# Tensor work of GpSimd moved to VectorE and ScalarE in a two-block transformer kernel, with paired matmul operands

## Chip, cores and metric

One core of one Trainium2 chip. The time is the device time of the core in microseconds (us). A change is read from the median of several runs; the stretches and waits are read from one profiled execution.

## The reference, cut to what matters

A model of two blocks over 256 tokens of width 1024, all inputs and results in float32. The first block has two layers with modulation by `c`: layer 0 with latent attention and retention over 512 tokens (256 of them context), layer 1 with an S5 state-space scan. The second has two layers, each with a gated feed-forward, a hybrid mixer (pooling and sparse attention) and a second feed-forward.

```python
def squared_relu_mlp(h, w1, w2):
    return jnp.square(jax.nn.relu(h @ w1)) @ w2
def swiglu(x, w_gate, w_up, w_down):
    return (jax.nn.silu(x @ w_gate) * (x @ w_up)) @ w_down
...
# first_block, layer l = 0, 1
    o_c, o_l = mla_retention_mixer(...) if l == 0 else s5_mixer(...)
    x = x + mod_l[:, 2] * o_l
    x = x + mod_l[:, 5] * squared_relu_mlp(h_l, mlp_w1[l], mlp_w2[l])
...
# second_block, layer l = 0, 1
    x = layer_norm(ALPHA * x + 0.5 * swiglu(x, ffn1...), ln1_g[l], ln1_b[l])
    x = layer_norm(ALPHA * x + hybrid_mixer(x, ...), ln2_g[l], ln2_b[l])
    x = layer_norm(ALPHA * x + 0.5 * swiglu(x, ffn2...), ln3_g[l], ln3_b[l])
```

## The kernel before, in words

Activations lie transposed: features on partitions, in 8 tiles of 128, tokens along the free axis. Weights come in units of 128 x 1024 float32 (512 KB, "raw"), each loaded by one DMA on SP's queue (L350, up to six ahead). For a product that keeps float32's accuracy each operand is split in two parts that the matmul engine takes: for a weight ScalarE casts the high part `whi` (L365) and the low part is `wlo = raw - whi` (L370); for an activation there are `xh` and `xl` in two tiles. `mm3` (L333) then issues three matmuls into one PSUM tile: `whi` with `xh`, `whi` with `xl`, `wlo` with `xh`. In a trace the stationary operand is the second name: `ps<-xl,whi`.

`wlo` is made on VectorE, or on GpSimd while the counter `s.n_pool` is above 0. It is set in four places: to 6 at the start, to 8 after the first pair of the first MLP (`fmulg`, L396) and after the first pair of each "raw" row of units (`raw_mul`, L437), to 7 in the hybrid mixer.

The raw row bridges a layer norm: while the norm's sums are still being made, PE multiplies the first eight units with the unnormalised activations (two more columns, 258, carry the correction), and `raw_norm` (L476, L477) corrects the result. `layernorm` (L1837) then makes per feature tile `lt`, `xh`, `xl` (L1868 to L1872) and, on GpSimd, `ax = ALPHA * y` (L1873) for the residual.

`ffn` (L1903) goes over 22 pairs of gate and up units: two products into two PSUM tiles, tanh on ScalarE, two VectorE operations (L1925, L1926), and a split into `hdh`, `hdl` (L719). Then eight output tiles of 22 products each, added to the residual in `resid` (L1888), whose sums over features go through `colacc` (L621), an add on GpSimd.

In layer 0 `l0_attn` (L993) makes, per head, a decay table for each of two shifts (`ret_table`) and the scores of retention (`ret_score`, a matmul with 64 rows). In layer 1 `s5_prep` makes norm sums, and eight scans run: `scan` multiplies by rotations (L1736, L1737), adds (L1740; one of the four adds on GpSimd), runs the recurrence (L1719) and in `post` rotates back on GpSimd (L1696 to L1699; the second half of the last scan on VectorE). `output` needs the matrices `s5km`, made earlier and kept in DRAM: 16 loads of 128 KB for its first part and 32 of 64 KB for its second, all on SP's queue (L1633); the second part's lie in buffers of `whi` and `wlo`.

The order of the instructions on each engine is set by a scheduler from the order in which the code is written and the buffers that are free; each engine then runs its own list in order.

Of the kernel before, what the change touches and what calls it, by code (L numbers as in the profile page):

```python
# [9 lines left out]
F32 = mybir.dt.float32  # L10
# [9 lines left out]
KT = D // 128  # L20
# [9 lines left out]
POOL_UNITS = 8  # L30
POOL_START = 6
# [7 lines left out]
POOL_ATT = 7  # L39
# [5 lines left out]
Z_POOL = (0, 1),  # L45
# [247 lines left out]

class K:
    def __init__(s, tc, A, out, voff, coff, ctx, dbg=None):
# [13 lines left out]
        s.n_dma = s.n_prep = s.n_use = s.n_pool = 0  # L309
# [48 lines left out]
    def _prep(s, i):  # L358
# [78 lines left out]
    def raw_mul(s, units):  # L437

        hi, lo, _ = s.xr
        for i in range(0, len(units), 2):  # L440
            w = [s.unit(*u) for u in units[i:i + 2]]
            ps = [s.ps([128, S + 2]) for _ in w]
            for k in range(KT):
                if i == 0 and k == KT - 1:
                    s.n_pool = POOL_UNITS
# [248 lines left out]
    def modnorm_raw(s, mk, x, st):  # L694
# [8 lines left out]
        out = [(mk(), mk()) for _ in range(KT)]  # L703
# [13 lines left out]
    def split(s, src, h, lw):  # L717
        s.nc.scalar.copy(h, src)
        s.nc.vector.tensor_tensor(lw, src, h, op=OP.subtract)  # L719
        return h, lw  # L720


    def layer0(s):
# [6 lines left out]
        with ExitStack() as es:  # L730
            slab = es.enter_context(tc.tile_pool(name="slab", bufs=43))
# [47 lines left out]
    def l0_proj(s, es, mx, x, halves):  # L779
# [9 lines left out]
        s.n_pool = POOL_START  # L789
# [94 lines left out]
        slab = es.enter_context(tc.tile_pool(name="slabq", bufs=9))  # L884
        s.rq, s.rk, s.sg = [], [], []
        for i in range(4, 12):
# [8 lines left out]
            nc.gpsimd.tensor_tensor(sh, sh, rs, op=OP.mult)  # L895
            V.tensor_tensor(dst[:, 0:S], dst[:, 0:S], rc, op=OP.mult)
            V.tensor_tensor(dst[:, 0:S], dst[:, 0:S], sh, op=OP.add)
            if i == 5:
# [3 lines left out]
                for n in range(3):  # L902
# [3 lines left out]
                    zs.append(s.split(zc[n], s.r2(), s.r2()))  # L906
# [30 lines left out]
        for hp in range(4):  # L937
# [5 lines left out]
            for a in range(2):  # L943
# [4 lines left out]
                nc.gpsimd.tensor_copy(k_[R], s.kr[R])  # L948
# [44 lines left out]
    def l0_attn(s, mx):  # L993
# [4 lines left out]
        dj = lambda jt: dd[:, 128 * (1 - jt):128 * (1 - jt) + S]  # L998
# [3 lines left out]
        def ret_table(h):  # L1002

            lf, lb = s.lg[:, 0, h:h + 1], s.lg[:, 0, 8 + h:9 + h]
            nb = s.lg[:, 1, 8 + h:9 + h]
            bf, bb = s.lg[:, 2, h:h + 1], s.lg[:, 2, 8 + h:9 + h]
            tbs[h] = []
            for jt in range(2):
                tb = s.r2(F32)
                t1 = s.sq.tile([128, S], F32, name="rt1", tag="shf")  # L1010
                t2 = s.sq.tile([128, S], F32, name="rt2", tag="rt2")
                V.tensor_scalar(t1, dj(jt), lf, None, op0=OP.mult)
                V.scalar_tensor_tensor(t1, in0=dj(jt), scalar=nb, in1=t1, op0=OP.mult, op1=OP.min)
                nc.scalar.activation(tb[:, S:], t1, AF.Exp)
                nc.scalar.activation(tb[:, 0:S], dj(jt), AF.Exp, scale=lf, bias=bf)
                nc.scalar.activation(t2, dj(jt), AF.Exp, scale=nb, bias=bb)
                nc.gpsimd.tensor_tensor(tb[:, 0:S], tb[:, 0:S], t2, op=OP.add)
                tbs[h].append(tb)

        def ret_score(h, jt):  # L1020
            hp, a = divmod(h, 2)
            r = slice(64 * a, 64 * a + 64)
            n = T2 if jt >= 2 else S
            ps = s.ps()
            s.mm(ps[:, :n], s.rk[hp][r, jt * 128:(jt + 1) * 128], s.rq[hp][r, :n])
# [44 lines left out]
        def mla_pv(hp):  # L1070
# [8 lines left out]
            ohl[hp] = s.split(po, s.r2(), s.r2())  # L1079
# [31 lines left out]
        for hp in range(4):  # L1111
# [7 lines left out]
            ohl[4 + hp] = s.split(s.sg[hp], s.r2(), s.r2())  # L1119
# [3 lines left out]
    def mlp(s, l, x, T, halves, fill=iter(()), st=None):  # L1123
        nc, tc = s.nc, s.tc
        m = s.mod[l]
        with ExitStack() as es:
# [4 lines left out]
            hp = eh.enter_context(tc.tile_pool(name="hm", bufs=16))  # L1131
            mk = lambda: hp.tile([128, T], F32R, name="hm", tag="hm")
# [8 lines left out]
            for c in range(32 // nf):  # L1141
                hid = []
                for f in range(nf):
# [9 lines left out]
                    elif l == 0 and c == 0 and f < 2:  # L1153
# [3 lines left out]
                        ps = first[f]  # L1157
                    else:
# [50 lines left out]
                for d in range(KT if l else 0):  # L1209
                    ps = s.ps()  # L1210
                    for f in range(nf):
# [3 lines left out]
                        s.mm3(ps[:, :T], (hi[:, o:o + 128], lo[:, o:o + 128]), hid[f], f == 0, f == nf - 1)  # L1215
                    for c0, c1, mi in halves:
                        nc.vector.scalar_tensor_tensor(x[:, d, c0:c1], in0=ps[:, c0:c1], scalar=m[:, 5, d, mi:mi + 1],
                                                       in1=x[:, d, c0:c1], op0=OP.mult, op1=OP.add)
# [1197 lines left out]
```

## Time and profile before

| | us |
|---|---|
| median of 3 runs | 2234.01 (2230.95 to 2234.57) |
| the profiled execution | 2235.03 |
| its span | 2233.2 |
| PE busy in it | 2050.1 (92%) |
| VectorE (DVE) busy | 1548.9 (69%) |
| ScalarE (ACT) busy | 996.7 (45%) |
| GpSimd (POOL) busy | 426.7 (19%) |

The span is the time from the first to the last instruction in the trace; 1.8 us lie around it. "Busy" counts the time in which at least one instruction of the engine runs. In a timeline a row stands for one instruction or for several of a kind that follow each other (xN), with its start, the time it took, and in brackets how long the engine had been idle and what it waited for. PEclk is the clock granted to the matmul engine as a share of full speed, 2.4 GHz; its lower level is 0.5.

### The profile page before, as it was taken

The numbers are of one execution on the slowest core, as the hardware profiler recorded it, in microseconds if no ns is written. First come the engines' busy times: TensorE is split into PE (matmuls) and PEld (weight loads), VectorE is DVE, ScalarE is ACT, GpSimd is POOL, SyncE is SP. The second block draws the span as 40 slices with busy tenths as digits, with TensorE's granted clock in tenths as the row PEclk, the third lists the DMA queues.
The fourth block names the chain that finished last, engine by engine and source line by source line (L and its number), as shares of the span: only waits on it lengthen the run. The fifth ranks groups of instructions, "written<-read, shape, count | busy, mean of one in ns | idle before, by whom it ended". The sixth has DMA issues, their size and how long they took to land. (4 is left out here: it accounts for less than half of the span.)

```text
span 2233.2 us, 39543 instructions
## 1 busy us (share of the span) xinstructions
PE 2050.1 (92%) x15641; PEld 1765.2 (79%) x15641; DVE 1548.9 (69%) x2880; ACT 996.7 (45%) x1808; POOL 426.7 (19%) x363
## 2 busy tenths in 40 slices
PE   6999998799997986899999998998999999798998
PEld 4774365577775875799999997788998999768996
DVE  6877666999873459775546558867658666878655
ACT  3443543233332343467434444545445444554443
POOL 2020114200000015540000024252024003426000
PEclk8999998899999997899999999999999999999999
DMA  7323433576778347245555555235553556314553
GB/s 292 109 78 125 158 105 131 188 214 223 237 231 251 125 160 247 99 160 192 185 183 182 180 191 160 86 104 167 184 198 133 192 192 200 127 39 170 189 182 121
DMA packets 137434, 373.67 MB, mean 167 GB/s; under 512 B 12896, under 2 KB 43552, under 8 KB 136736
## 3 DMA queue, kind: packets, MB, share of 16 engines
q1 hardware_dynamic: 137248, 371.14, 50.4%
q8 instruction: 123, 2.02, 0.4%
q14 instruction: 63, 0.52, 0.1%
HBM read 345.33 MB, written 25.76 MB: 166 GB/s over the span
## 5 line engine op out<-in xcount | busy, mean ns | idle before, releaser
L365 ACT CAST whi<-raw 128x1024 fp32r<-128x1024 f32 (+1 forms) x491 | 510.7, 1044 | 641.5 <-PE ps L323 406.9
L370 DVE TENSOR_TENSOR wlo<-raw,whi 128x1024 fp32r<-128x1024 f32 (+1 forms) x407 | 507.6, 1248 | 391.0 <-ACT whi L365 390.9
L323 PE MATMUL ps<-xl,whi 128*128 128x256 f32 x1312 | 375.2, 286 | 12.2 <-DVE xl L1872 12.2
L323 PE MATMUL ps<-xh,whi 128*128 128x256 f32 x1312 | 379.1, 289 | 3.5 <-ACT whi L365 2.5
L323 PE MATMUL ps<-xh,wlo 128*128 128x256 f32 x1312 | 372.2, 284 | 2.8 <-POOL wlo L370 2.8
L323 PEld LDWEIGHTS ps<-xl,whi 128*128 128x128 f32 x1312 | 251.4, 192 | 16.3 <-DVE xl L1872 14.6
L370 POOL TENSOR_TENSOR wlo<-raw,whi 128x1024 fp32r<-128x1024 f32 (+1 forms) x84 | 214.0, 2561 | 236.0 <-ACT whi L365 132.1
L323 PEld LDWEIGHTS ps<-xh,whi 128*128 128x128 f32 x1312 | 251.5, 192 | 7.4 <-ACT whi L365 3.3
L323 PEld LDWEIGHTS ps<-xh,wlo 128*128 128x128 f32 x1312 | 251.1, 192 | 3.5 <-POOL wlo L370 3.5
L323 PE MATMUL ps<-hm,whi 128*128 128x512 f32 (+1 forms) x896 | 231.4, 350 | 0.4 <-ACT lt L1497 0.4
L323 PE MATMUL ps<-hidh,whi 128*128 128x512 f32 (+1 forms) x512 | 174.8, 345 | 12.2 <-ACT whi L365 11.0
L323 PEld LDWEIGHTS ps<-hm,whi 128*128 128x128 f32 x896 | 155.6, 190 | 29.2 <-issue 3.1
L323 PE MATMUL ps<-hidl,whi 128*128 128x512 f32 (+1 forms) x512 | 174.7, 341 | 2.3 <-DVE hidl L719 2.1
L323 PE MATMUL ps<-hidh,wlo 128*128 128x512 f32 (+1 forms) x512 | 172.5, 338 | 0.0
L323 PE MATMUL ps<-hm,wlo 128*128 128x512 f32 (+1 forms) x448 | 155.0, 346 | 5.0 <-POOL wlo L370 5.0
L323 PE MATMUL ps<-hdl,whi 128*128 128x256 f32 x528 | 149.1, 283 | 0.0
L323 PE MATMUL ps<-hdh,whi 128*128 128x256 f32 x528 | 148.5, 282 | 0.0
L323 PE MATMUL ps<-hdh,wlo 128*128 128x256 f32 x528 | 148.4, 281 | 0.0
L323 PE MATMUL ps<-slab,whi 128*128 128x512 f32 x416 | 133.1, 399 | 1.5 <-ACT slabq L931 1.5
L323 PEld LDWEIGHTS ps<-hidh,whi 128*128 128x128 f32 x512 | 97.0, 190 | 27.1 <-ACT whi L365 11.9
L323 PE MATMUL ps<-xrh,whi 128*128 128x258 f32 x384 | 110.6, 290 | 0.0
L323 PE MATMUL ps<-xrl,whi 128*128 128x258 f32 x384 | 109.4, 287 | 0.0
(539 smaller groups left out, 4313.9 us busy)
## 6 DMA issues: line engine op xcount, KB each, us to landing
raw<-in_m_dram SPq DMA_DIRECT2D x128, 512.0 KB, 4.3
raw<-in_f1gu_dram SPq DMA_DIRECT2D x88, 512.0 KB, 3.5
raw<-in_f2gu_dram SPq DMA_DIRECT2D x88, 512.0 KB, 3.7
raw<-in_ada_dram SPq DMA_DIRECT2D x80, 512.0 KB, 4.3
raw<-in_f1d_dram SPq DMA_DIRECT2D x44, 512.0 KB, 3.8
raw<-in_f2d_dram SPq DMA_DIRECT2D x44, 512.0 KB, 3.7
raw<-in_ni_dram SPq DMA_DIRECT2D x24, 512.0 KB, 3.5
slab<-in_adaq_dram SPq DMA_DIRECT2D x32, 256.0 KB, 6.2
```

Source lines behind the costliest of these rows:

```text
L323: s.last = s.nc.tensor.matmul(out, lhsT, rhs, start=start, stop=stop)
L365: nc.scalar.copy(hi[:, :w], raw[:, :w])
L370: eng.tensor_tensor(lo[:, :w], raw[:, :w], hi[:, :w], op=OP.subtract)
```

## The change

1. All `wlo` are made on VectorE; the counter goes. `colacc`, the sums of `s5_prep`, the scan's add and `post`, the rotary products and the decay table's add go from GpSimd to VectorE. `ax`, a copy of the rotary keys and two fills of `s5M` go to ScalarE.
2. `xh` and `xl` of an activation lie side by side in one tile (`HL`). Where the PSUM tile has three dimensions, `mm3` issues one 512-column matmul of `whi` with both and one of 256 columns of `wlo` with `xh`; the two halves are added afterwards, by `both` (a ScalarE copy and a VectorE add) or by two residual operations. This holds for the gate and up units that are not raw, for the down projections but the last feed-forward's, and for the second MLP's units from the ninth on with its down projection. Layer 0, the raw units, the projections and the last down projection stay as they were.
3. In layer 0 both shifts' decay tables are one tile, made for one head in one set of operations, and `ret_score` issues the matmuls of a pair of heads one after the other.
4. The loads of `s5km` go from SP's queue to GpSimd's.

```diff
     def mm3(s, out, w, x, start, stop):
+        if len(out.shape) == 3:
+
+            s.mm(out, w[0], x.both, start, False)
+            s.mm(out[:, 0], w[1], x[0], False, stop)
+            return
...
-        eng = nc.gpsimd if s.n_pool > 0 else nc.vector
-        s.n_pool -= 1
-        eng.tensor_tensor(lo[:, :w], raw[:, :w], hi[:, :w], op=OP.subtract)
+        nc.vector.tensor_tensor(lo[:, :w], raw[:, :w], hi[:, :w], op=OP.subtract)
...
-            s.nc.gpsimd.tensor_tensor(acc[0], acc[1] if d == 1 else acc[0], v, op=OP.add)
+            s.nc.vector.tensor_tensor(acc[0], acc[1] if d == 1 else acc[0], v, op=OP.add)
...
+    def both(s, ps, t):
+
+        s.nc.scalar.copy(t, ps[:, 1])
+        s.nc.vector.tensor_tensor(t, ps[:, 0], t, op=OP.add)
+        return t
...
-        def ret_score(h, jt):
-            hp, a = divmod(h, 2)
-            r = slice(64 * a, 64 * a + 64)
+        def ret_score(hp, jt):
...
+            pss = [s.ps() for _ in range(2)]
+            for a, ps in enumerate(pss):
+                r = slice(64 * a, 64 * a + 64)
+                s.mm(ps[:, :n], s.rk[hp][r, jt * 128:(jt + 1) * 128], s.rq[hp][r, :n])
...
+                    elif l:
+                        ps = s.ps([128, 2, T])
+                        s.fmul(ps, f"m1_{l}", f, h)
+                        ps = s.both(ps, s.sq.tile([128, T], F32, name="hb"))
...
-                nc.gpsimd.tensor_tensor(acc, acc, sq, op=OP.add)
+                nc.vector.tensor_tensor(acc, acc, sq, op=OP.add)
...
-                s.nc.sync.dma_start(w[j::8].rearrange("p a b x -> p (a b) x"), src[0:16, :, 16 * j:16 * j + 128])
+                s.nc.gpsimd.dma_start(w[j::8].rearrange("p a b x -> p (a b) x"), src[0:16, :, 16 * j:16 * j + 128])
...
-                post(i, Y, R, slice(0, 8), G)
+                post(i, Z, R, slice(0, 8))
...
-                nc.gpsimd.tensor_scalar(ax[:, k], t, b[:, k:k + 1], ALPHA, op0=OP.add, op1=OP.mult)
+                nc.scalar.activation(ax[:, k], t, AF.Identity, bias=ba[:, k:k + 1], scale=ALPHA)
...
-        nc.vector.scalar_tensor_tensor(r[:, d], in0=ps, scalar=f, in1=ax[:, d], op0=OP.mult, op1=OP.add)
+        z = ax[:, d]
+        for p in (ps[:, 1], ps[:, 0]) if len(ps.shape) == 3 else (ps,):
+            nc.vector.scalar_tensor_tensor(r[:, d], in0=p, scalar=f, in1=z, op0=OP.mult, op1=OP.add)
+            z = r[:, d]
...
-                    pg, pu = s.ps([128, S]), s.ps([128, S])
+                    pg, pu = s.ps([128, 2, S]), s.ps([128, 2, S])
                     s.fmulg([(z, f"f{f}gu_{l}", 2 * i + n) for n, z in enumerate((pg, pu))], x, early=KT)
+                    pg, pu = (s.both(z, s.sq.tile([128, S], F32, name=f"gu{n}", bufs=2)) for n, z in enumerate((pg, pu)))
```

How the order of the instructions moves, at three places. First PE in the first down projection (the activations `hdh`, `hdl`), before:

```order
L323 MATMUL ps<-hdh_11456,whi 128x256
L323 MATMUL ps<-hdl_11457,whi 128x256
L323 MATMUL ps<-hdh_11456,wlo 128x256
L323 MATMUL ps<-hdh_11526,whi 128x256
L323 MATMUL ps<-hdl_11527,whi 128x256
L323 MATMUL ps<-hdh_11526,wlo 128x256
```

and now, where the tile `hdh` holds both parts:

```order
L328 MATMUL ps<-hdh_10954,whi 128x512
L328 MATMUL ps<-hdh_10954,wlo 128x256
L328 MATMUL ps<-hdh_11013,whi 128x512
L328 MATMUL ps<-hdh_11013,wlo 128x256
L328 MATMUL ps<-hdh_11072,whi 128x512
L328 MATMUL ps<-hdh_11072,wlo 128x256
```

Two of three 256-column products became one of 512 columns; the third stays.

Second VectorE on the way from a layer norm into a feed-forward (`lt` and `xl` of the norm, `rawt` and `th` of the raw units), the last rows up to the last `xl`, before:

```order
L1869 SCALAR_TENSOR_TENSOR lt<-lt,vec,ps 128x256
L1868 TENSOR_TENSOR lt<-x_126,ps 128x256
L476 SCALAR_TENSOR_TENSOR rawt<-lbs,rawc,ps 128x256
L477 TENSOR_TENSOR rawt<-rawt,lbs 128x256
L1926 SCALAR_TENSOR_TENSOR th<-th,rawt 128x256
L1872 SCALAR_TENSOR_TENSOR xl_15463<-lt,vec,xh_15462 128x256
L1869 SCALAR_TENSOR_TENSOR lt<-lt,vec,ps 128x256
L1872 SCALAR_TENSOR_TENSOR xl_15465<-lt,vec,xh_15464 128x256
L477 TENSOR_TENSOR rawt<-rawt,lbs 128x256
L719 TENSOR_TENSOR hdl_15623<-th,hdh_15622 128x256
L1925 SCALAR_TENSOR_TENSOR th<-th,rawt 128x256
L1872 SCALAR_TENSOR_TENSOR xl_15467<-lt,vec,xh_15466 128x256
```

and now (`xl` is the second half of the tile `xh`, written at L1903):

```order
L479 SCALAR_TENSOR_TENSOR rawt<-lbs,rawc,ps 128x256
L1903 SCALAR_TENSOR_TENSOR xh_14544<-lt,vec,xh_14544 128x256
L1960 SCALAR_TENSOR_TENSOR th<-th,rawt 128x256
L480 TENSOR_TENSOR rawt<-rawt,lbs 128x256
L1900 SCALAR_TENSOR_TENSOR lt<-lt,vec,ps 128x256
L377 TENSOR_TENSOR wlo<-raw,whi 128x1024
L480 TENSOR_TENSOR rawt<-rawt,lbs 128x256
L1961 SCALAR_TENSOR_TENSOR th<-th,rawt 128x256
L479 SCALAR_TENSOR_TENSOR rawt<-lbs,rawc,ps 128x256
L377 TENSOR_TENSOR wlo<-raw,whi 128x1024
L430 SCALAR_TENSOR_TENSOR xrl<-vec,xrh 128x8 x2
L1903 SCALAR_TENSOR_TENSOR xh_14545<-lt,vec,xh_14545 128x256
```

Low parts of weights, which were on GpSimd's list, now stand between the norm's operations, six of them from the first correction to the last `xl`.

Third the loads of `s5km`: SP's queue before (`m_0` is the first MLP's weights, `s5w`, `s5R`, `s5c` are scan weights),

```order
L1633 DMA s5km<-s5ld 16x16x128 x6
L350 DMA raw<-in_m_0_dram 128x1024 x2
L1633 DMA s5km<-s5ld 16x16x128 x10
L350 DMA raw<-in_ada_dram 128x1024 x2
L350 DMA raw<-in_m_0_dram 128x1024 x18
L350 DMA raw<-in_wglu_dram 128x1024 x2
L1610 DMA s5w<-s5wd 128x2x512
L1610 DMA s5c<-s5cd 128x2x512 x8
L1610 DMA s5w<-s5wd 128x2x512 x3
L1633 DMA s5km<-s5ld 16x8x128 x32
L1610 DMA s5w<-s5wd 128x2x512 x7
```

and GpSimd's queue now:

```order
L1456 MEMSET bb 128x512 x8
L1580 COPY s5ot<-ident 128x1024
L1661 DMA s5km<-s5ld 16x16x128 x16
L1661 DMA s5km<-s5ld 16x8x128 x18
L1716 MEMSET s5M_7422 128x8
L1716 MEMSET s5M_7424 128x8
L1661 DMA s5km<-s5ld 16x8x128 x14
```

SP's list no longer has them; on GpSimd's 18 of the second part's 32 stand ahead of the memsets of `s5M`, which the first recurrences read.

## Rows read from the trace of the kernel before

**Rows 1.** The page's first part: busy time of each engine over the span.

```profile
PE 2050.1 (92%) x15641; PEld 1765.2 (79%) x15641; DVE 1548.9 (69%) x2880; ACT 996.7 (45%) x1808; POOL 426.7 (19%) x363
```

**Rows 2.** Windows: length, engines' busy us, granted clock, DMA share, GB/s.

```profile
350.00:450.00 100.00, 75.58 (x404) 50.12 (x403) 90.49 (x178) 28.36 (x51) 29.84 (x11) 0.84 0.51 166
1340.00:1475.00 135.00, 118.61 (x1104) 99.59 (x1103) 103.71 (x250) 70.03 (x185) 49.16 (x40) 0.95 0.36 112
1760.00:1860.00 100.00, 100.00 (x846) 100.00 (x845) 60.65 (x81) 46.58 (x67) 6.96 (x6) 1.00 0.57 190
1200.00:1300.00 100.00, 100.00 (x836) 100.00 (x835) 59.28 (x84) 47.46 (x70) 0.77 (x2) 1.00 0.58 186
```

**Rows 3.** PE's waits by releaser: total us, times, longest us.

```profile
PE ps L323 <- ACT x L1703: 15.0, 4, 6.4
PE ps L323 <- ACT whi L365: 13.5, 4, 11.0
...
PE ps L323 <- DVE xl L1872: 12.2, 9, 2.2
PE ps L323 <- ACT qq L2060: 11.4, 4, 5.5
...
PE ps L323 <- POOL wlo L370: 7.8, 4, 5.0
...
PE ps L323 <- POOL racc L624: 5.3, 2, 2.7
```

**Rows 4.** Timeline of DVE, 1493 to 1523 us: start, us, engine, line, operation.

```profile
1494.11 0.48 DVE L476 SCALAR_TENSOR_TENSOR rawt<-lbs,rawc,ps 128x256 f32<-128x256 f32 x1 [4.44 <-ACT lbs L1860]
...
1495.23 2.42 DVE L477 TENSOR_TENSOR rawt<-rawt,lbs 128x256 f32<-128x256 f32 x1
...
1508.89 0.41 DVE L477 TENSOR_TENSOR rawt<-rawt,lbs 128x256 f32<-128x256 f32 x1
...
1520.29 2.59 DVE L1872 SCALAR_TENSOR_TENSOR xl<-lt,vec,xh 128x256 fp32r<-128x256 f32 x1
```

**Rows 5.** Timeline of POOL beside it.

```profile
1517.55 5.04 POOL L370 TENSOR_TENSOR wlo<-raw,whi 128x1024 fp32r<-128x1024 f32 x2
```

**Rows 6.** Timeline of PE in a row of 512-column matmuls, the first and the 20th.

```profile
659.67 0.39 PE L323 MATMUL ps<-hidh,whi 128*128 128x512 f32 x1
...
663.99 0.39 PE L323 MATMUL ps<-hidl,whi 128*128 128x512 f32 x1
```

**Rows 7.** The page's fifth part: low parts on VectorE and GpSimd.

```profile
L370 DVE TENSOR_TENSOR wlo<-raw,whi 128x1024 fp32r<-128x1024 f32 (+1 forms) x407 | 507.6, 1248 | 391.0 <-ACT whi L365 390.9
...
L370 POOL TENSOR_TENSOR wlo<-raw,whi 128x1024 fp32r<-128x1024 f32 (+1 forms) x84 | 214.0, 2561 | 236.0 <-ACT whi L365 132.1
```

**Rows 8.** Timeline of SP's queue around the loads of `s5km`.

```profile
688.09 7.72 SPq L1633 DMA_DIRECT2D s5km<-s5ld  x6
697.76 3.10 SPq L350 DMA_DIRECT2D raw<-in_m_dram  x2
...
821.90 22.42 SPq L1633 DMA_DIRECT2D s5km<-s5ld  x32
```

**Rows 9.** Timeline of DVE in the S5 scans.

```profile
845.82 0.74 DVE L1740 TENSOR_TENSOR s5Z<-s5Z,s5t 128x256 f32<-128x256 f32 x2
...
847.09 2.32 DVE L1719 TENSOR_TENSOR_SCAN s5Z<-s5M,s5Z 128x512 f32<-128x512 f32 x2
...
870.22 2.77 DVE L1719 TENSOR_TENSOR_SCAN s5Z<-s5M,s5Z 128x512 f32<-128x512 f32 x2
...
888.00 0.66 DVE L1736 TENSOR_TENSOR s5Z<-ps,s5R 128x512 f32<-128x512 f32 x1
888.58 0.67 DVE L1737 TENSOR_TENSOR s5t<-ps,s5R 128x512 f32<-128x512 f32 x1
...
893.48 2.33 DVE L1719 TENSOR_TENSOR_SCAN s5Z<-s5M,s5Z 128x512 f32<-128x512 f32 x2
```

**Rows 10.** PE by form: the 512-column matmuls with 64 rows.

```profile
L323 PE MATMUL ps<-slab 64*128 64x512 f32 x32 | 18.0, 641 | 0.0
```

More of the change, by code (lines that the diff above doesn't have):

```diff
@@ L290, in unit_order, with __new__ @@
     return u
+class HL(tuple):
+    def __new__(cls, t):
+        o = super().__new__(cls, (t[:, 0], t[:, 1]))
+        o.both = t
+        return o
 class K:
@@ L702, in modnorm_raw @@
         s.xn = None, bs
-        out = [(mk(), mk()) for _ in range(KT)]
+        out = [HL(mk()) for _ in range(KT)]
         def apply():
@@ new lines, in ret_table @@
+            t1, t2 = (s.sq.tile([128, 384], F32, name="rt" + n, tag="rt" + n, bufs=1) for n in "12")
+            V.tensor_scalar(t1, dd, lf, None, op0=OP.mult)
+            V.scalar_tensor_tensor(t1, in0=dd, scalar=nb, in1=t1, op0=OP.mult, op1=OP.min)
+            nc.scalar.activation(tb[:, 1], t1, AF.Exp)
+            nc.scalar.activation(tb[:, 0], dd, AF.Exp, scale=lf, bias=bf)
+            nc.scalar.activation(t2, dd, AF.Exp, scale=nb, bias=bb)
+            V.tensor_tensor(tb[:, 0], tb[:, 0], t2, op=OP.add)
@@ L1214, in mlp @@
                         o = f % 8 * 128
[L1215 to L1218, printed above, removed]
-                    nc.gpsimd.tensor_scalar(x[:, d, S:T2], x[:, d, 0:S], ALPHA, None, op0=OP.mult)
-                    s.xs.append(s.split(x[:, d, 0:S], *(s.xp.tile([128, S], F32R, name=f"x{n}{d}", tag=f"x{n}{d}")
-                                                        for n in "hl")))
+                        s.mm3(ps, (hi[:, o:o + 128], lo[:, o:o + 128]), hid[f], f == 0, f == nf - 1)
+                    for i in (1, 0):
+                        nc.vector.scalar_tensor_tensor(x[:, d, 0:S], in0=ps[:, i], scalar=m[:, 5, d, 0:1],
+                                                       in1=x[:, d, 0:S], op0=OP.mult, op1=OP.add)
+                    nc.scalar.activation(x[:, d, S:T2], x[:, d, 0:S], AF.Copy, scale=ALPHA)
+                    s.xs.append(s.split(x[:, d, 0:S], s.pair(s.xp, f"xh{d}")))
                 if c == 6 and l == 0:
@@ L1541, in s5_tables @@
         for f in range(2):
[L1542 to L1543 removed]
+            yield from s.s5_km_steps(0, f, 4)
     def s5_prep(s, x, on):
@@ L1624, in s5_load_km, with s5_km_steps @@
     def s5_load_km(s, i, f):
+        for _ in s.s5_km_steps(i, f, 8):
+            pass
+    def s5_km_steps(s, i, f, step):
         km = []
@@ L1688, in layer1, with post @@
         X = {}
-        def post(i, Y, R, gs, E):
+        def post(i, Y, R, gs):
             n = gs.stop - gs.start
@@ L1709, in scan @@
             M = mt[i % 2]
-            (G.tensor_copy if i < 2 else nc.scalar.copy)(M[:, :, 1:64], s.s5rho[:, 8 * i:8 * i + 8].unsqueeze(2).to_broadcast([128, 8, 63]))
+            nc.scalar.copy(M[:, :, 1:64], s.s5rho[:, 8 * i:8 * i + 8].unsqueeze(2).to_broadcast([128, 8, 63]))
             if i >= 4:
@@ L1794, in layer1 @@
         hp = es2.enter_context(tc.tile_pool(name="s5h", bufs=1, side="right"))
-        hl = [(hp.tile([128, S], F32R, name=f"s5h{k}"), hp.tile([128, S], F32R, name=f"s5l{k}")) for k in range(KT)]
+        hl = [s.pair(hp, f"s5h{k}") for k in range(KT)]
         for hf in range(2):
@@ L1861, in layernorm @@
         s.xn = bs[:, :, 0], bs[:, :, 1]
+        ba = s.sm.tile([128, KT], F32, name="lba")
+        V.tensor_scalar(ba, b, ALPHA, None, op0=OP.mult)
         ax = s.ax
-        out = [tuple(pool.tile([128, S], F32R, name=f"x{n}{k}", tag=f"x{n}{k}") for n in "hl") for k in range(KT)]
+        out = [s.pair(pool, f"xh{k}") for k in range(KT)]
         def apply():
```

114 lines of the change are left out of this document (51 added, 63 removed).

## The prediction, made before the change was run

> **What bounds the kernel now.** I read the busy shares first, then the windows by stage, then what the matmul engine (PE) waits for, then single stretches of the timeline. PE is busy 2050.1 of 2233.2 us [rows 1]; the reader should see that no other engine comes near. The windows say where that mean is made of two kinds of stage [rows 2]: in the feed-forward stretches PE is busy 100.00 of 100 us while VectorE has 60.65, so there only fewer or shorter matmuls count; in 350 to 450 us and 1340 to 1475 us PE stands still for 24.4 and 16.4 us and VectorE is busy 90.49 of 100 and 103.71 of 135 us, so there VectorE sets the pace. The ledger of PE's waits [rows 3] puts names on the 183 us that PE is idle: 13.1 us ended directly by GpSimd (7.8 for low parts `wlo`, 5.3 for norm sums `racc`), 12.2 us by VectorE's `xl`, 13.5 us by a cast whose transfer was late, 15.0 us in the scans' outputs. GpSimd alone bounds little. What it does to VectorE counts: while it runs, VectorE instructions with two SBUF inputs stretch [rows 4]: the same L477 product took 2.42 and 0.41 us, an `xl` 2.59 us, beside two `wlo` of GpSimd's that took 5.04 us [rows 5].
>
> The Trainium skill ("SBUF — State Buffer", Who interferes with whom) says the same of two SBUF inputs against a GpSimd instruction that reads SBUF: one blocks the other fully. By that rule all of the blocked time comes back; the sum below takes back only what a wait of PE rests on.
>
> **The change part by part.** All is set against the profiled execution, 2235.0 us, 1.0 us above the median of 2234.0. Measuring tells this kernel from no change at about 0.2%, 4.5 us.
>
> *Fused matmuls.* Three 256-column products become one of 512 and one of 256. The triples: 44+36+36+36 gate/up units of 8 (1216), 3 x 8 x 22 in the down projections (528), 24 x 8 and 8 x 32 in the second MLP (448); 2192 in all. In steady state a 256-column matmul starts every 100/846 = 0.118 us in the feed-forward and 100/836 = 0.120 us in the MLP [rows 2]; a 512-column one every 4.32/19 = 0.227 us [rows 6]. A triple saves 0.009 or 0.012 us: 1744 x 0.009 + 448 x 0.012 = 21 us. Bounds: nothing if a 512 behind a 256 costs both starts, 28 us if the saving is 0.013 everywhere. I take **-21**. The halves must then be added: per gate/up unit one ScalarE copy and one VectorE add (about 0.4 us each by the small rows of [rows 4]), two per pair. VectorE's 60.65 us of 100 leave 39 for about 18 pairs, so 18 x 0.8 = 14 us lie under PE; if that cover went, it would be a wait of 0.8 us per pair.
>
> *Low parts on VectorE.* 84 `wlo` leave GpSimd (214.0 us) and cost VectorE 84 x 1.25 = 105 us [rows 7]. They are worth something only in the transitions. *Into the feed-forward, three times*: VectorE's chain from the first L476 to the last `xl` ran from 1494.11 to 1522.88, 28.8 us [rows 4]. By the new order it holds 43 small operations, which follow each other every 0.37 us unblocked [rows 9], and six `wlo` of 1.25 [rows 7]: 15.9 + 7.5 = 23.4. The last `xl` comes 5.4 us sooner; two of the three also lose the 2.7 us wait for `racc` [rows 3]. That is 22 us at most; ScalarE's casts come next in line, so I take **-16** (-8 to -22). *Into the mixer, twice*: 15 `wlo` (19 us) come to VectorE, which was busy 103.71 of 135 us [rows 2] with part of that blocked; PE waits there mainly on chains (`qq` 11.4 us in all [rows 3]). Gain and cost nearly balance; **-8** (0 to -20). *First MLP, 350 to 450*: eight `wlo` go from GpSimd, one of which ended the longest wait for it, 5.0 us [rows 3]; of the 24 us that PE idles there I take **-11** (-5 to -14). *Start*: six `wlo` and a few norm sums, **-2** (+1 to -3).
>
> *Loads of `s5km`.* On SP, six issues of 128 KB took 7.72 us and stood ahead of two weight loads issued at 697.76 [rows 8], ten more right behind those. PE then waited 11.0 us for a cast of late weights, the longest of the 13.5 us [rows 3]. On GpSimd's own queue they no longer stand ahead of anything on SP. The bytes are the same, so some contention stays: **-9** (-4 to -12). Later 32 issues of 64 KB took 22.42 us of SP [rows 8], with seven scan weights behind them; VectorE, not those weights, paced the scans, so I cost that at nothing.
>
> *S5 scans.* The scan's products after the recurrence go to VectorE. Before, the scan pairs started at 870.22 and 893.48 with three periods between: 7.75 us each [rows 9]. After, one scan holds four products of 0.58 (start to start), four adds of 0.37, the recurrence pair of 2.33 and a post of 2 x 0.58 + 2 x 0.37 = 1.9 us: 8.0 us without any blocking [rows 9]. Seven periods cost 2 to 3 us, the last half scan's post (1.3 us, was GpSimd's) 1 us, six norm sums before it 1 to 2 us: **+6** (+1 to +9). Behind it the splits of the output are unblocked: **-1**.
>
> *Retention.* Scores of the two heads of a pair now stand next to each other, on rows 0 to 63 and 64 to 127 of the array. The 512-column ones are half of the 32 matmuls with 18.0 us [rows 10], 9.0 us, and as many of 256 columns cost less; side by side they would cost half. No row shows such a pair adjacent: bounds 0 and -8, I take **-4**, the middle. The shared table saves ScalarE and VectorE work that PE did not wait for: nothing.
>
> *Rotary products, ALPHA scaling to ScalarE, memsets*: ScalarE is busy 45% and VectorE 69% [rows 1]; nothing, within 2 us either way.
>
> Sum: -21 - 16 - 8 - 11 - 2 - 9 + 6 - 1 - 4 = -66 us; 2235.0 - 66 = 2169 on the profiled execution, **2168** on the median.
>
> **Rivals.** *(1) The waits only change owner.* VectorE takes 105 us of `wlo` and some 25 us of sums and products for about as much blocked time given back; each transition then ends when it did. For it: VectorE is at 90% in 350 to 450 [rows 2]. Against: the counted feed-forward chain is shorter. Left are the matmuls, the loads and the two `racc` waits: -21 - 9 - 5 + 6 = -29, 2205 us.
>
> *(2) All of the blocked time comes back, and the clock with it.* In 350 to 450 the granted clock was 0.84, so about 32 us were at the lower level, 1.2 GHz, each time behind an idle PE; in 1340 to 1475 it was 0.95 [rows 2]. Every term at its far end: -28 - 22 - 20 - 14 - 3 - 12 + 1 - 2 - 8 = -108, 2126 us. For it: a wait that goes takes its slow stretch along. Against: chains such as `qq` on ScalarE stay.
>
> *(3) Slower: the GpSimd queue is late.* In the new order GpSimd issues 18 of the 32 later `s5km` loads ahead of two memsets of `s5M`, without which the first recurrence cannot start. SP's issues began at 821.90 and that recurrence at 847.09 [rows 8, 9]: 25.2 us for 18, 1.4 us each; SP took 0.70. Beyond 1.4 us every extra us per issue costs 18 us, and 5.1 us per issue eats the whole -66. For it: no issue on GpSimd's queue stands in any row, so its price is open. Against: GpSimd has nothing else to do there. At 6 us it is +17, 2251 us. The Trainium skill ("SBUF — State Buffer", Who interferes with whom) speaks against the change here: descriptors that GpSimd writes itself can be starved while VectorE holds the shared port in its two-port modes. No row here shows it; it would make rival 3.
>
> *(4) A 512-column product saves nothing* and the additional adds hold PSUM banks: the first term is 0, the rest stays: 2189 us; inside the range.
>
> **How the numbers follow.** Forecast with its neighbourhood (2140 to 2190, rival 4 included): 0.62. Rival 1 (2190 to 2225): 0.2. Rival 2 (below 2140): 0.11. Rival 3: 0.07, of which 0.02 lies within 0.2% of 2234 and 0.04 above it, the rest below. The range 2128 to 2208 leaves out the far end of rival 2, the upper part of rival 1 and rival 3, together about 0.2. Faster by over 0.2%: 0.94; within: 0.02; slower: 0.04.
>
> **What would show it.** Fused: 512-column starts with `whi` about 0.227 us apart from the next, PE still at 100% there and some 1% fewer us per unit. Transitions: no VectorE operation of 256 columns above 0.7 us, L480 at 0.41, PE's wait for `xl` shorter by some 5 us per transition, none for GpSimd. Loads: the gap at 707 us gone or a few us. Scans: recurrence pairs about 8.0 us apart. Retention: pairs of score matmuls starting together. The prediction is wrong if `s5M`'s memsets come later than the first recurrence would, if VectorE's chain into the feed-forward still takes 28 us, or if the feed-forward stretches stop being PE's.

## The result and the profile after

The changed kernel took 2181.07 us (median of 4 runs, 2179.94 to 2185.06), the kernel before on the same chip 2232.48 (2229.16 to 2234.57): a ratio of 0.978 [0.977, 0.980], 51 us faster. That is inside the range and 13 us above the forecast of 2168. The profiled execution has a span of 2178.6 us, 54.6 less than before. Its first part answers to [rows 1]:

```profile
PE 2022.9 (93%) x13449; PEld 1643.5 (75%) x13449; DVE 1587.6 (73%) x3302; ACT 1061.8 (49%) x2018; POOL 41.6 (2%) x120
```

GpSimd is all but empty, VectorE has only 39 us more work although 105 us of low parts and the adds of the halves came to it, and PE is still the busiest. A low part costs on VectorE what it cost there before (1248 ns, now 1217), and less than half of GpSimd's 2561; in the fifth part ([rows 7]):

```profile
L377 DVE TENSOR_TENSOR wlo<-raw,whi 128x1024 fp32r<-128x1024 f32 (+1 forms) x491 | 597.0, 1217 | 350.8 <-ACT whi L375 347.9
```

What PE waits for, the rows that answer to [rows 3] and the new ones among the longest (in total, times, longest):

```profile
PE ps L328 <- ACT whi L375: 17.9, 4, 15.9
PE ps L328 <- ACT x L1733: 11.2, 4, 7.9
...
PE ps L328 <- DMA raw<-in_ada_dram: 10.9, 2, 6.9
...
PE ps L328 <- DVE xh L1903: 6.6, 6, 1.5
...
PE ps L328 <- ACT qq L2095: 2.1, 2, 1.0
...
PE ps L328 <- DVE wlo L377: 1.8, 3, 0.8
```

No wait on GpSimd is left. The waits for `xl` (now in `xh`) fell from 12.2 to 6.6 us, for `qq` from 11.4 to 2.1. But the cast of late weights, which was to shrink, grew from 13.5 to 17.9, and a wait of 6.9 us for a load is new.

To see where the time went I put the two traces side by side. Both cast the same 491 units of weights in the same order, so the start of the k-th cast of `whi` is a landmark; each line is by how much the distance between two landmarks changed, in us, against the term predicted:

| casts | what lies there | predicted | measured |
|---|---|---|---|
| 0 to 16, 24 to 32 | start, rest of the attention | -2 | -2.8 |
| 16 to 24 | retention | -4 | -13.3 |
| 32 to 42 | first MLP's start | -11 | -10.0 |
| 42 to 74 | layer 0's MLP | 0 | +7.2 |
| 74 to 96 | the stall in layer 0's MLP (described below); loads of `s5km` | -9 | +6.9 |
| 96 to 104 | S5 scans, output splits | +6, -1 | +2.7, -3.9 |
| from 104 | fused stretches | -21 | about -11 |
| 248 to 264, 400 to 424 | mixers | -8 | about -9.5 |
| 264 to 288, 336 to 352, 432 to 440 | transitions into a feed-forward | -16 | about -21 |

In the last three lines about a microsecond is moved from the transitions to the other two, since their first products are fused ones too; by the landmarks alone the three are -10.2, -9.2 and -22.1. All of it comes to -55, the spans' difference.

**Transitions.** VectorE's timeline of the same transition as in [rows 4]:

```profile
1468.69 0.48 DVE L479 SCALAR_TENSOR_TENSOR rawt<-lbs,rawc,ps 128x256 f32<-128x256 f32 x1 [2.24 <-ACT lbs L1889]
...
1469.81 0.42 DVE L480 TENSOR_TENSOR rawt<-rawt,lbs 128x256 f32<-128x256 f32 x1
...
1475.95 1.22 DVE L377 TENSOR_TENSOR wlo<-raw,whi 128x1024 fp32r<-128x1024 f32 x1
...
1490.66 0.47 DVE L1903 SCALAR_TENSOR_TENSOR xh<-lt,vec,xh 128x256 fp32r<-128x256 f32 x1
```

The product that took 2.42 us beside GpSimd takes 0.42 in every instance, and from the first L479 to the end of the last `xl` (L1903, 1491.13) it is 22.4 us where it was 28.8, with six low parts in between; the prediction had counted 23.4.

**The stall.** PE, and SP's and GpSimd's queues, where [rows 8] had SP alone:

```profile
694.09 0.79 PE L328 MATMUL ps<-hidh,whi 128*128 128x512 f32 x1 [15.95 <-ACT whi L375]
```

```profile
670.28 3.51 SPq L360 DMA_DIRECT2D raw<-in_m_dram  x2
```

```profile
663.58 4.59 POOL L1661 DMA_DIRECT2D s5km<-s5ld  x8 [22.84 <-DVE wlo L377]
671.37 0.56 POOL L1661 DMA_DIRECT2D s5km<-s5ld  x1 [3.20 <-DMA s5km<-s5ld]
...
809.21 9.44 POOL L1661 DMA_DIRECT2D s5km<-s5ld  x18 [127.80 <-PE ps L328]
818.63 0.17 POOL L1716 MEMSET s5M<- 128x8 f32 x2
```

SP now issues the two weight loads at 670.28 with no load of `s5km` before them, and yet PE stands still for 15.95 us until their cast. What the transfers did between 664 and 692 us, by queue and by issue (packets, MB, share of the 16 engines; then KB each and median us to landing):

```profile
q1 hardware_dynamic: 1967, 5.28, 68.3%
q0 software_dynamic: 768, 2.10, 32.6%
...
s5km<-s5ld POOLq DMA_DIRECT2D x16, 128.0 KB, 9.0
...
raw<-in_m_dram SPq DMA_DIRECT2D x2, 512.0 KB, 21.7
```

The engines are full, a third of them with GpSimd's queue, and the weights took 21.7 us to land where the page's median for such loads is 4.4. Within that window, from 675 to 680 us, the two queues take half each:

```profile
q1 hardware_dynamic: 288, 0.65, 53.5%
q0 software_dynamic: 212, 0.59, 50.4%
```

The second group of loads shows what one issue on GpSimd costs: 9.44 / 18 = 0.52 us, and the memsets came at 818.63, in time.

### The profile page after: what moved, and what is told of

It reads as the page before. It is cut to its first block, busy times and chain, and to the rows that moved or that the text cites. A ratio compares the mean times of both kernels' runs of the same rounds, so it can differ in the third digit from the quotient of the medians.

```text
span 2178.6 us, 35381 instructions
## 1 busy us (share of the span) xinstructions
PE 2022.9 (93%) x13449; PEld 1643.5 (75%) x13449; DVE 1587.6 (73%) x3302; ACT 1061.8 (49%) x2018; POOL 41.6 (2%) x120
## 5 line engine op out<-in xcount | busy, mean ns | idle before, releaser
L377 DVE TENSOR_TENSOR wlo<-raw,whi 128x1024 fp32r<-128x1024 f32 (+1 forms) x491 | 597.0, 1217 | 350.8 <-ACT whi L375 347.9
L328 PE MATMUL ps<-xh,whi 128*128 128x512 f32 (+1 forms) x1408 | 465.0, 383 | 8.8 <-DVE xh L1903 6.6
L328 PE MATMUL ps<-hm,whi 128*128 128x512 f32 x704 | 228.7, 396 | 0.8 <-DVE x L1227 0.8
L328 PE MATMUL ps<-hdh,whi 128*128 128x512 f32 x528 | 186.4, 397 | 0.0
L328 PE MATMUL ps<-hidh,whi 128*128 128x512 f32 x256 | 102.1, 406 | 19.9 <-ACT whi L375 16.5
L328 PEld LDWEIGHTS ps<-hdh,whi 128*128 128x128 f32 x528 | 99.0, 188 | 24.2
L328 PE MATMUL ps<-xrh,wlo 128*128 128x258 f32 x384 | 109.5, 288 | 0.0
L328 PE MATMUL ps<-hidl,whi 128*128 128x512 f32 x256 | 102.0, 399 | 5.7 <-DVE hidl L723 5.7
L328 PE MATMUL ps<-hidh,wlo 128*128 128x512 f32 x256 | 101.6, 400 | 0.5 <-DVE wlo L377 0.5
L328 PEld LDWEIGHTS ps<-hdh,wlo 128*128 128x128 f32 x528 | 99.1, 188 | 0.3
L328 PEld LDWEIGHTS ps<-slab,whi 128*128 128x128 f32 x416 | 78.3, 190 | 18.5 <-issue 1.0
```

The lines of the kernel that those rows point to most:

```text
L328: s.last = s.nc.tensor.matmul(out, lhsT, rhs, start=start, stop=stop)
L377: nc.vector.tensor_tensor(lo[:, :w], raw[:, :w], hi[:, :w], op=OP.subtract)
```

## The experiments

The kernel before took 2230.4 to 2230.6 us beside them (medians). The changed kernel was not run again there; beside it the kernel before had taken 2232.5, so differences of 2 us against the change mean nothing. Steps between landmarks are against the changed kernel unless another is named, and come from one profiled execution each.

**The loads of `s5km` back on SP**, the rest as changed.

```diff
-                s.nc.gpsimd.dma_start(w[j::8]...
+                s.nc.sync.dma_start(w[j::8]...
```

> The changed kernel (2181 us) with one part undone: the loads of s5km are issued on SP's queue again. Burst theory (in the changed profile the DMA engines are full from 664 to 692 us, because GpSimd's queue gets about half of their time and the weights on SP wait for it): the first part's loads share one queue with the weights again, the wait of 16.0 us at 694 us falls to about 11 us as before the change, 2174 to 2178 us. Order theory (the prediction's: loads ahead of the weights on SP cost 9 us): the wait grows, 2188 to 2192 us.

2176.52 us (2175.99 to 2177.68), ratio 0.975 [0.974, 0.977]: 4.5 us faster than the change; between casts 72 and 80 it is 5.4 us shorter. PE's and SP's rows, and the transfers in the same window of 664 to 692 us:

```profile
688.67 0.80 PE L328 MATMUL ps<-hidh,whi 128*128 128x512 f32 x1 [9.16 <-ACT whi L375]
```

```profile
669.50 7.61 SPq L1661 DMA_DIRECT2D s5km<-s5ld  x6
678.54 2.92 SPq L360 DMA_DIRECT2D raw<-in_m_dram  x2
```

```profile
q1 hardware_dynamic: 5936, 7.26, 96.4%
...
raw<-in_m_dram SPq DMA_DIRECT2D x2, 512.0 KB, 8.6
```

SP issues the weights 8.3 us later than in the changed kernel, behind six loads of `s5km`, and they land earlier: 8.6 us after the issue, not 21.7. The window moves the same bytes (7.26 MB against 5.28 + 2.10), so the bytes did not go away; their order did. On one queue ten of the sixteen `s5km` come behind the weights; on two queues most of them move beside the weights. The Trainium skill ("DMA: Bandwidth & Descriptors", SWDGE vs HWDGE vs iDMA) says that software and hardware queues feed different queues of each DMA engine, which alternates between them; the shares of 53.5% and 50.4% between 675 and 680 us agree that both were served at once.

**The same loads written later in the program**, still on GpSimd.

```diff
-        for f in range(2):
-            yield from s.s5_km_steps(0, f, 4)
...
+                            if d < 4:
+                                s.s5_load_km(0, d // 2)
```

> The changed kernel with the 16 loads of s5km for the first part issued about 90 us later, in the last pass of layer 0's MLP, still on GpSimd's queue. Burst theory: 2 MB leave the full stretch, the wait at 694 us falls from 16.0 to 4 to 9 us, and nothing is late at the first output (864 us): 2169 to 2175 us. Order theory: SP's list is the same as in the changed kernel, so no change: 2179 to 2183 us.

2183.29 us (2179.17 to 2186.35), 0.978 [0.977, 0.980]: no difference from the change. The reason is in GpSimd's rows:

```profile
662.94 4.57 POOL L1661 DMA_DIRECT2D s5km<-s5ld  x8 [21.74 <-DVE wlo L377]
```

The loads went out at 662.94, where they had gone at 663.58, and not 90 us later: GpSimd's list is so short that a later place in the program is no later time. The experiment did not do what it was for, and says nothing for or against the burst. A version with these loads late on SP, or all behind the two weight loads, wasn't run.

**The products not fused**, the pair tiles and all else as changed.

```diff
-                    pg, pu = s.ps([128, 2, S]), s.ps([128, 2, S])
+                    pg, pu = s.ps([128, S]), s.ps([128, S])
...
-                    pg, pu = (s.both(z, ...) for n, z in enumerate((pg, pu)))
...
-                ps = s.ps([128, 2, S])
+                ps = s.ps([128, S])
```

(and the same for the second MLP's two products).

> The changed kernel with the paired operands unfused: three 256-column products per weight tile again and no adds of halves. By the intervals in the changed profile (512 followed by 256: 0.233 + 0.119 us against 3 x 0.119 to 0.120) 2192 triples save 5 to 7 ns each: 11 to 15 us, so 2192 to 2196 us. As predicted (0.009 to 0.012 us each): 2202 us. If the additional adds cost what the products save: 2179 to 2183 us.

2172.94 us (2172.59 to 2175.29), 0.974 [0.972, 0.976]: 8 us faster than fused; none of the expected values. Windows of 50 us (columns as in [rows 2]), PE fully busy in all, tell half of it. The first of each pair lies in the first down projection (activations `hdh`), the second in the gate and up units of the third feed-forward (activations `xh`). Before:

```profile
1288.00:1338.00 50.00, 50.00 (x419) 50.00 (x419) 29.28 (x31) 22.97 (x32) 11.89 (x11) 1.00 0.57 190
1750.00:1800.00 50.00, 50.00 (x424) 50.00 (x423) 29.76 (x44) 23.99 (x36) 0.00 (x0) 1.00 0.57 189
```

Changed, fused:

```profile
1268.00:1318.00 50.00, 50.00 (x285) 43.45 (x284) 32.96 (x49) 23.55 (x31) 0.00 (x0) 1.00 0.61 193
1705.00:1755.00 50.00, 50.00 (x287) 43.80 (x286) 36.52 (x62) 28.68 (x53) 0.00 (x0) 1.00 0.61 184
```

Not fused:

```profile
1262.00:1312.00 50.00, 50.00 (x443) 50.00 (x443) 32.05 (x45) 24.22 (x33) 0.00 (x0) 1.00 0.61 202
1697.00:1747.00 50.00, 50.00 (x423) 50.00 (x422) 30.21 (x44) 23.68 (x35) 0.00 (x0) 1.00 0.55 181
```

The first number in brackets counts PE's products. A triple is the work of one weight tile: three products before and without fusion, two when fused. In the down projection: 50 / 419 x 3 = 0.358 us before, 50 / 285 x 2 = 0.351 fused, 50 / 443 x 3 = 0.339 not fused. In the gate and up units: 0.354, 0.348, 0.355. (Products that lie only partly in a window are counted too, about two, so these times are 1 to 3 ns low; the differences hardly change.) So fusing gains 6 ns per triple for `xh` and loses 12 for `hdh`, because an unfused product with `hdh` now starts every 0.113 us, not 0.119. By these, not fusing is worth 976 x 12 - 1216 x 6 ns = 4 us of the 8 (976 triples of `hdh` and of the second MLP's `hm` and `hid`, 1216 of `xh`); the rest is spread over the span, and no row names it. Nothing in the diff explains why the unfused product became faster. What differs between the two kernels is the place of the tiles: in the allocation, `hdh`, `hm` and `hid` lay at a byte address of 96 modulo 128 in their partitions before, as the weights `whi` and `wlo` do, and lie at 32 now, because two new small tiles (`lba`) shifted them by 64 bytes. The next three kernels try that.

**The kernel before with an unused tile of 64 bytes** ahead of these buffers.

```diff
+        s.padl = e(tc.tile_pool(name="padl", bufs=1)).tile([128, 16], F32, name="padl")
+        s.nc.vector.memset(s.padl, 0.0)
```

> The kernel before with nothing but an unused 64-byte tile after the small tiles, which shifts hm, hidh, hidl, hdh and hdl by 64 bytes (from 96 to 32, modulo 128, in each partition; the weights stay at 96, xh and xl too). Address theory: 256-column products on these tiles start every 113 ns and no longer every 119 to 120, those on xh stay at 119: 976 triples x 3 x 6 ns = 18 us less, layer 0's 512-column ones 1 to 2 ns more (+3 us): 2213 to 2218 us. Pairing theory (the 113 ns in the unfused kernel come from high and low part lying in one tile): no change, 2228 to 2235 us.

2225.49 us (2215.60 to 2229.70), 0.997 [0.996, 0.999]: faster by 0.3%, less than expected. The down projection's window:

```profile
1285.00:1335.00 50.00, 50.00 (x443) 50.00 (x443) 30.98 (x33) 24.38 (x33) 13.75 (x12) 1.00 0.62 197
```

443 products where there were 419, by 64 unused bytes. In the second MLP the product started every 0.118 us, down from 0.120, not 0.113. The third down projection did the same, although its tiles have the addresses of the first:

```profile
1819.00:1869.00 50.00, 50.00 (x427) 50.00 (x426) 28.95 (x33) 23.31 (x31) 11.20 (x10) 1.00 0.57 195
```

So at this distance a stretch runs at 0.113 or at 0.118 us per product, and why less in some is open. That is one reason for the gain of 5 us in place of 13 to 18.

**Not fused, and `xh` shifted by 64 bytes too.**

```diff
+        s.padr = e(tc.tile_pool(name="padr", bufs=1, side="right")).tile([128, 16], F32, name="padr")
+        s.nc.vector.memset(s.padr, 0.0)
```

> The unfused kernel with a 64-byte tile at the other end of SBUF, which shifts xh (both parts) from 96 to 32 modulo 128. Address theory: the gate and up products fall from 119 to 113 ns as well: 1216 x 3 x 5.5 ns = 20 us less than the unfused 2173: 2150 to 2156 us. Pairing theory: 2170 to 2176 us.

2168.68 us (2166.08 to 2170.47), 0.972 [0.970, 0.974]: 4 us less, not the 20 expected. The windows of the first and second down projection and of the gate and up units:

```profile
1262.00:1312.00 50.00, 50.00 (x444) 50.00 (x443) 32.60 (x45) 24.18 (x32) 0.00 (x0) 1.00 0.60 202
1583.00:1633.00 50.00, 50.00 (x427) 50.00 (x426) 30.68 (x41) 22.73 (x32) 0.00 (x0) 1.00 0.59 196
1697.00:1747.00 50.00, 50.00 (x427) 50.00 (x426) 31.06 (x45) 23.25 (x37) 0.00 (x0) 1.00 0.55 186
```

With `xh` 427 products start where 423 did: about 1 ns less for each, which over 3648 products is the 4 us. So the address counts a little for `xh` too, but it gets the slower of the two paces, as the second down projection does here.

**Not fused, and the weights shifted by 64 bytes instead**, the activations where they were (two unused tiles).

```diff
+        s.padw = e(tc.tile_pool(name="padw", bufs=1)).tile([128, 16], F32, name="padw")
+        s.nc.vector.memset(s.padw, 0.0)
```

> The unfused kernel with the weights' tiles at 32 modulo 128 and the activations where they were (hid, hdh, hm at 32, xh at 96). If the distance between weight and activation counts: products on hid and hdh rise from 113 to 119 ns, those on xh fall from 119 to 113; about 2169 us. If the activation's own address counts: intervals as in the unfused kernel, 113 and 119, and 2171 to 2175 us.

2190.26 us (2186.32 to 2192.23), 0.982 [0.980, 0.984]: 17 us slower than without the shift. The down projection:

```profile
1276.00:1326.00 50.00, 50.00 (x419) 50.00 (x418) 29.27 (x40) 22.88 (x30) 0.00 (x0) 1.00 0.57 190
```

419 again. The activations hadn't moved modulo 128, so it isn't their own address but the one against the weights': the same modulo 128 is slow, 64 bytes apart is faster. The 976 triples at 3 x 6 to 7 ns make 18 to 20 us; `xh`, which is now 64 bytes from the weights, gives some 4 us back, and 17 were measured. The Trainium skill ("TensorE: Matmul & The Clock Gate", Step-by-step: what each phase is for) says that the streamed operand and the weight loads have independent read ports, and that loading weights takes no bandwidth from the running product. By that the distance of the two addresses should not matter; here it does, and the measurement decides. By what mechanism it matters no run shows.

**Low parts back on GpSimd**, by the counter as before; the rest as changed.

```diff
-        nc.vector.tensor_tensor(lo[:, :w], raw[:, :w], hi[:, :w], op=OP.subtract)
+        eng = nc.gpsimd if s.n_pool > 0 else nc.vector
+        s.n_pool -= 1
+        eng.tensor_tensor(lo[:, :w], raw[:, :w], hi[:, :w], op=OP.subtract)
```

> The changed kernel with the low parts of 84 units on GpSimd again (the counters of the kernel before), all else as changed. If blocking of VectorE by GpSimd is what the transitions lost: three transitions into the feed-forward 5 to 7 us each longer and two into the mixer 3 to 5 us, the first MLP's start 5 to 10 us: 2205 to 2215 us. If the waits only change owner (rival 1): 2178 to 2186 us.

2221.39 us (2215.99 to 2226.98), 0.996 [0.994, 0.997]: 40 us lost again. In the profiled execution, the longest of the six, the landmarks move by 14 us up to cast 96, 4 in each mixer, 7 to 9 in each transition into a feed-forward, and by 0.0 in most steady stretches. Against the kernel before, the two mixers and the three transitions (the third from cast 424) are then as long as they were, within half a microsecond. VectorE's and GpSimd's rows in the transition:

```profile
1508.16 2.12 DVE L486 TENSOR_TENSOR rawt<-rawt,lbs 128x256 f32<-128x256 f32 x1
1510.21 2.62 DVE L1968 SCALAR_TENSOR_TENSOR th<-th,rawt 128x256 f32<-128x256 f32 x1
```

```profile
1507.43 5.12 POOL L379 TENSOR_TENSOR wlo<-raw,whi 128x1024 fp32r<-128x1024 f32 x2 [3.34 <-ACT rawc L479]
```

The slow operations are back, where no other tensor work of GpSimd's is. That is the cause of most of the gain, and rival 1 falls: the waits did not just change owner. In mixers and transitions the low parts are the whole of it; the sums, `ax` and the other work that also left GpSimd give nothing there by themselves.

**The S5 scans' products back on GpSimd** (`post`, one add in four, the fills).

```diff
-                    V.tensor_tensor(Z[:, c, gs], t1[:, c], t2[:, c], op=op)
+                    E = G if (f, c) == (0, 1) and i < 7 else V
+                    E.tensor_tensor(Z[:, c, gs], t1[:, c], t2[:, c], op=op)
...
-                post(i, Z, R, slice(0, 8))
+                post(i, Z, R, slice(0, 8), G)
```

> The changed kernel with the S5 scan's products after the recurrence, one add and two fills of s5M on GpSimd again. If VectorE paces the scans and blocking is smaller than the work moved (prediction: +5 for the scans; the two traces: 62.7 us from the first product to the last post after, 59.7 before): 2175 to 2179 us. If GpSimd blocks VectorE by as much as it relieves it: 2180 to 2184 us.

2181.01 us (2177.51 to 2183.87), 0.977 [0.976, 0.979]: the same; from cast 96 to 104 0.9 us more. What VectorE is spared it loses on the operations that stay with it. Its adds in the scans, with the shortest, the median and the longest in ns, in this run and in the changed kernel:

```profile
L1770 DVE TENSOR_TENSOR s5Z<-s5Z,s5t x25: 413/716/1431, 832.7 to 895.0; 128x256 f32<-128x256 f32 x25
L1769 DVE TENSOR_TENSOR s5Z<-s5Z,s5t x32: 411/416/426, 830.4 to 892.3; 128x256 f32<-128x256 f32 x32
```

In the changed kernel's scans two recurrence pairs follow each other by 7.84 us, where [rows 9] had 7.75 and the prediction 8.0:

```profile
852.25 2.33 DVE L1749 TENSOR_TENSOR_SCAN s5Z<-s5M,s5Z 128x512 f32<-128x512 f32 x2
...
860.09 2.33 DVE L1749 TENSOR_TENSOR_SCAN s5Z<-s5M,s5Z 128x512 f32<-128x512 f32 x2
```

**Retention's scores one head at a time.**

```diff
-                if i % 2:
-                    ret_score(h // 2, (2, 3, 0, 1)[i % 8 // 2])
+                ret_score(h // 2, (2, 3, 0, 1)[i % 8 // 2], i % 2)
```

> The changed kernel with the retention scores of the two heads of a pair issued apart, each with one of the two attention steps that the pair had, tables as changed. Side-by-side theory (the 64-row matmuls took 26.7 us start to start before and 14.9 us after): about 12 us return, 2190 to 2195 us. If the merged tables made the gain in this stage: 2179 to 2184 us.

2201.08 us (2197.43 to 2202.72), 0.986 [0.985, 0.988]: 20 us slower. PE's matmuls with 64 rows by form (busy us, mean ns of one), changed, and with the heads apart:

```profile
L328 PE MATMUL ps<-slab 64*128 64x512 f32 x32 | 10.1, 641 | 0.0
...
L328 PE MATMUL ps<-slab 64*128 64x256 f32 x32 | 6.0, 428 | 0.0
```

```profile
L328 PE MATMUL ps<-slab 64*128 64x512 f32 x32 | 18.0, 641 | 0.0
...
L328 PE MATMUL ps<-slab 64*128 64x256 f32 x32 | 11.1, 428 | 0.0
```

One takes 641 or 428 ns in both, but the 64 of them cover 16.1 us in place of 29.1: next to each other the two heads run side by side. The steps are 9.5 us between casts 16 and 24, 3.4 to cast 32, and some 11 us in pieces later that no row explains (1.4 us less before cast 16).

**More work for VectorE in both MLPs**: one add per hidden tile whose result nobody reads, of 128x512 in layer 0 and of 128x256 in layer 1.

```diff
+                    if not s.xr or f >= RAW:
+                        nc.vector.tensor_tensor(r[:, :T], q[:, :T], ab[0], op=OP.add)
```

> The changed kernel with one more VectorE add per hidden tile in both MLPs, whose result nobody reads: 32 of 0.7 us in layer 0, 24 of 0.4 us in layer 1. If VectorE paces layer 0's MLP from 370 to 640 us (and so took back the 10 us won at its start): 10 to 17 us more there and nothing in layer 1, 2191 to 2198 us. If PE or the transfers pace it: at most 3 us more, 2180 to 2185 us.

2181.93 us (2173.51 to 2183.91), 0.977 [0.975, 0.979]: no change, though VectorE is busy 12.6 us more in 240 us of layer 0's MLP:

```profile
440.00:680.00 240.00, 233.35 (x1468) 174.13 (x1466) 208.13 (x402) 83.32 (x138) 13.77 (x22) 0.99 0.73 226
```

In the changed kernel:

```profile
440.00:680.00 240.00, 229.41 (x1459) 171.02 (x1457) 195.50 (x382) 80.50 (x137) 11.74 (x21) 1.00 0.74 223
```

So VectorE does not pace this stretch. What took back 7 us there (casts 42 to 74 in the table) is better seen in PE's waits: 15.5 us in the changed kernel, 7.4 before. The largest:

```profile
421.71 1.92 PE L328 MATMUL ps<-raw,sc 128*32 128x512 f32 x4 [6.89 <-DMA raw<-in_ada_dram]
```

Before, all waits in this stretch for loads of `ada`, the weights of the modulation by `c`, were these (total, times, longest):

```profile
PE ps L323 <- DMA raw<-in_ada_dram: 2.9, 2, 2.1
```

So 4 of the 7 us are work that is earlier and waits for a load that is not; the rest lies in waits for ScalarE and VectorE. What holds the load was not tried, so this account is argued and not shown.

**The best of both, in two forms**: nothing fused, `xh` shifted, loads on SP; and only the gate and up units fused, loads on SP (the edits shown above).

> A version meant to be better than both: unfused, xh shifted as well, and the s5km loads on SP's queue. Address theory and burst theory together: 2173 - 20 - 4.5 = 2144 to 2152 us. If the shift does nothing: 2166 to 2170 us.

2162.51 us (2158.52 to 2162.87), 0.969 [0.967, 0.971].

> A version meant to be better than both: only the gate and up products stay fused (their triples took 351 ns fused and 356 to 360 unfused), the down projections and the second MLP are unfused (353 fused, 340 unfused), s5km's loads on SP. Interval theory: 2173 - 4.5 - 6 = 2160 to 2165 us. If the adds of the halves cost what the fused gate and up products save: 2166 to 2171 us.

2161.55 us (2159.56 to 2169.41), 0.970 [0.967, 0.972]. The two can't be told apart; both are 19 to 20 us (0.9%) faster than the change. In the second the steps against it are -7.1 between casts 72 and 80 and -0.9 per eight units of weights in the second MLP and the down projections.

## Why the prediction was right, and where not

*The ground of it held.* VectorE's blocked operations were the cost, and the transitions were where it showed. "-16" for the feed-forward was about -21 and "-8" for the mixers about -9.5; the counted chain of 23.4 us measured 22.4. The undoing of this one part costs 40 us, against 51 for the whole change. The first MLP's start gave 10 of 11. One part of the reasoning did not hold: the two waits for `racc` were counted into the transitions, but with the sums on VectorE and only the low parts back on GpSimd the transitions are as long as before.

*Fused matmuls, "-21", were about -11.* The step that failed is the saving per triple: 9 to 12 ns were taken from a 512-column product following its like (0.227 us), but alternating with a 256 the pair took about 0.35 us, 6 to 7 ns less than three products took before. The -11 lies midway between the forecast and rival 4, in which it saves nothing. And for `hdh`, `hid` and `hm` the comparison with before is not one of fusing at all: at the new addresses the unfused form is the faster by 12 ns per triple.

*Loads of `s5km`, "-9", came out at +7 with all else between the casts 74 and 96.* The mechanism was wrong. The step was "on GpSimd's own queue they no longer stand ahead of anything on SP"; in its place the runs show that transfers of two queues take the same engines at the same time, and that SP's order had kept ten of the sixteen behind the weights. Back on SP it is 4.5 us faster, 5.4 by the landmarks, so the move itself cost about 5 of the 7; the rest is not explained. "Some contention stays" was the right sentence with the wrong size.

*Retention, "-4", measured -13.* The middle was taken between 0 and a bound that was itself too small: only half of the 32 products of 512 columns were counted as scores, but all 64 matmuls of [rows 10] and its sister of 256 columns are, and side by side they cost 16.1 us in place of 29.1.

*Layer 0's MLP, no term at all, gave back 7 us.* So of the 10 us won at its start 3 were left. What earlier work meets was not priced: waits for loads of `ada` grew from 2.9 to 6.9 us, and the other 3 us lie in waits for ScalarE and VectorE.

*S5 scans, "+6", were +2.7, and the splits, "-1", -3.9.* The period of 7.84 us was below the 8.0 worked out, and the run with the products on GpSimd shows the two placements equal within the noise.

*Rival 3 is dead* with 0.52 us per issue against a turning point of 1.4. The Trainium skill ("SBUF — State Buffer", Who interferes with whom) warned of descriptors that are starved while VectorE works in its two-port modes; while the 18 went out (809 to 826 us) VectorE was busy 12.58 of 17 us and each issue took 0.52 us; before the stall it was busy 2.08 of 18.5 us and each took 4.59 / 8 = 0.57. So none is seen here; whether any of VectorE's work then was in such a mode, no row says. *Rival 2* asked for all terms at their far ends; retention and the splits went past theirs, but the fused products came to half of the forecast and the loads fell on the other side of zero.

That the total came within 13 us is in good part luck, for it rests on errors that cancel: 10 and 16 us too hopeful for the fused products and the loads, 7 for layer 0's MLP, against 9 too careful for retention, 6 for scans and splits, 5 for the transitions into feed-forwards and 1.5 for the mixers.

## What to carry to other kernels

Before handing tensor work to GpSimd, look in VectorE's timeline for the same operation with two very different durations; what GpSimd does beside it is paid for by VectorE, and matters in the stages in which VectorE sets the pace. A transfer on a second queue is not out of the way of the first: ask which bytes must land first, and put the others behind them on the same queue. When a fused product or a new small tile changes a stretch that is all PE, test the unfused form in the new layout too, before crediting the fusion.

## What the runs showed of the hardware that was not expected

- When the activations' address equals the weights' modulo 128 bytes, a 128x256 product starts every 0.119 to 0.120 us; when they are 64 bytes apart, every 0.113 or every 0.118: 419 to 424 products in 50 us against 443 or 427, switched by unused tiles in both directions. Which of the two it is at 64 bytes is not explained: `hdh` has mostly 0.113, `xh` always 0.118, and the down projections of one run have both at the same addresses.
- A 512-column product followed by one of 256 with other weights takes about 0.35 us for the two.
- Two products of 64 rows, on different halves of the array and next to each other in PE's list, overlap nearly fully: 64 of them cover 16.1 us instead of 29.1, and apart from each other they cost the kernel 20 us.
- An issue of `s5km` on GpSimd takes 0.52 us for 64 KB and 0.57 for 128 KB, where SP took 22.42 / 32 = 0.70 and 7.72 / 6 = 1.29 [rows 8].
